# Deferred low parts in three norms, early gains, and a new order of three projections in a two-layer transformer kernel

## The chip, the cores and the metric

The kernel runs on one core of a Trainium2 chip. The metric is the device time of one execution in microseconds (us), the lower the better. The engines are named as in the profile: PE is TensorE (its weight loads are shown as PEld), DVE is VectorE, ACT is ScalarE, POOL is GpSimd, and SP is SyncE, which issues most of the DMAs. A queue name with a q at its end (SPq, POOLq) is the sequencer of that engine.

## The reference, cut to what matters

Two layers run one after the other on 512 tokens of 1024 features. The first mixes a sparse attention with a state-space scan. The second mixes a band attention with a gated delta rule and ends in a retrieval of experts (PEER). Three places matter here.

```python
def modulate(h, shift, scale):                    # and the same in layer 1
    return h * (1.0 + scale) + shift
h = modulate(rms_norm_2(x, norm1_gain), shift1, scale1)      # norm of layer 2
h2 = modulate(rms_norm_2(x, norm2_gain), shift2, scale2)     # norm before PEER
proj = h @ w_in                                   # qa, ka, va, qkv_b, z_b, ...
o_a = chunked_band_attention(qa, ka, va, ...)     # norms qa and ka per head, then attends
o_att = sparse_attention(...) * jax.nn.silu(z_att)           # layer 1, 8 heads
```

In the band attention the queries and the keys are normalized per head of 64; the values go in as they are. The gated delta rule needs, for each tile of 128 tokens, the inverse of a unit triangular matrix for each of its four heads.

## The kernel before, in words

**Products in three parts.** Every matrix product keeps float32 accuracy with three passes: a matrix is split into a high part (`hi`, `wh`) and a low part (`lo`, `wl`), and PE multiplies high by high, high by low and low by high. `wload` (L57) loads a block of weights into one of four `wr` buffers through SP, ACT copies the high part (L51), and DVE subtracts it to get the low part (L52), or POOL does if `eng` says so. There are three buffers for each part, so splits run up to three blocks ahead of their products. `gemm_t` (L76) gives a transposed result with 512 columns to each product (L72 to L74); `gemm_n` (L87) gives one row tile of 128 tokens to each of four PSUM buffers "g", of which the pool has four (L98 to L100). `gemm_n` walks over four blocks of weights with four row tiles in each, 96 products in all, and calls `mid` after every second row tile, eight times in all.

**Norms.** `norm_mod` (L210) runs three times: at the start of layer 1 (8 blocks of 128 features, fed while the modulation weights still arrive: `pre(k)` multiplies two of their blocks, L194), at the start of layer 2, and before PEER. For each block k it makes `y` (L220, DVE), the high part (L221, ACT) and the low part (L222, DVE, which needs the high part). There are three buffers for `y`. Layer 2 loads its gain at its own start (L883) and multiplies it with the modulation (L884); the norm before PEER does the same (L1273, L1274).

**Layer 1, attention.** `ssd_pre` makes eight projections with their low parts on POOL. Beside them DVE runs the top-k rounds of the indexer (L483, L484), which `pump` hands out. Then `att1_head` (L516) runs for eight heads, each beginning with a `gemm_t` of `w_za`.

**Layer 2, band projections.** `dn_pre` makes the delta rule's projections, `dn_tiles([0, 1])` inverts the matrices of the first two tiles, and `band_pre` (L1166) makes the three band projections with `gemm_n` while it hands out the rounds of `dn_tiles([2, 3])` through `mid`. One round is one step of both tiles. There are 19 with work in them: five that build the matrices, twelve that alternate between L1054 (with the transposes L1043) and L1063 for six levels, counting the first transpose, then the last results L1068 and L1074. Before: half the values (`w_va1`, 256 columns, 0.5 of a round per call), then queries and keys (512 columns each, 0.9 of a round per call). Each of the last two ends with a chain for four row tiles: copy out of PSUM (L1194, ACT), square (L1196), sum (L1198), power of -0.5 on POOL (L151), multiply (L1200), all in buffers "cv_u" and "cv_t", two each. `trans` (L1177) then transposes on PE (L1181) and copies with a scale (L1183). The queries are transposed after the keys' products; the keys' transposes are tied behind the last L1054 (`issue_after`).

**After that.** `band` (L1205) loads a bias for each head (L1215; POOL writes a corner, L1216), multiplies queries by keys (L1220) and runs a softmax on DVE and ACT (`soft`, L534), interleaved with the scan of the delta rule.

**What sets the order.** The code is a program without waits. At build time a planner fixes the order of the instructions on each engine: by its own estimate of durations it takes, at each moment, the ready instruction that stands earliest in the program. On the chip each engine runs its own list in order and waits where an input is late. The order in the program is thus a priority, not yet the order that runs.

Of the kernel before, what the change touches and what calls it, by code (L numbers as in the profile page):

```python
# [8 lines left out]
F32 = mybir.dt.float32  # L9
# [5 lines left out]
AF = mybir.ActivationFunctionType  # L15
OP = mybir.AluOpType
# [4 lines left out]
P = 128  # L21
T = 512
NT = 4
# [3 lines left out]
class Kernel:  # L27
# [181 lines left out]

    def norm_mod(self, pool, xs, hs, G, shift, ss, pre=None, mid=None):  # L210


        nc = self.nc
        r = self.rstd_bcast(pool, ss, 1.0 / 1024, "nm", pre is None, mid)
        for k in range(8):
            y = self.t(pool, [P, T], F32, "nm_y", 3)
            hi, lo = hs[k]
            if pre is not None:
                pre(k)
            nc.vector.scalar_tensor_tensor(y, xs[k], G[:, k:k + 1], r, op0=OP.mult, op1=OP.mult)  # L220
            nc.scalar.activation(hi, y, AF.Identity, bias=shift[:, k:k + 1])  # L221
            nc.vector.scalar_tensor_tensor(lo, y, shift[:, k:k + 1], hi.bitcast(F32), op0=OP.add, op1=OP.subtract)  # L222

    def run(self):
        tc, nc = self.tc, self.nc
# [133 lines left out]
    def att1_pre(self, hs):  # L359
        tc, nc, I = self.tc, self.nc, self.i  # L360
        ap, a0 = self.ap, self.ap0
        self.rope_tables(a0)
        G = nc.gpsimd

# [150 lines left out]

    def att1_head(self, h, hs):  # L516
        nc, ap = self.nc, self.ap
        z = self.gemm_t(self.i["w_za"][h], 8, hs)
        tz = self.t(ap, [P, T], F32, "tz", 1)
        nc.scalar.activation(tz, z, AF.Tanh, scale=0.5)  # L520
        zz = self.t(ap, [P, T], F32, "zz", 2)
        nc.vector.scalar_tensor_tensor(zz, tz, 1.0, z, op0=OP.add, op1=OP.mult)
        kv = h // 4
        o = self.t(self.pa, [P, T], F32, "a")
        for i in range(NT):
            N = P * (i + 1)
            s = self.t(self.pa, [P, T], F32, "a")[:, :N]
            nc.tensor.matmul(s, self.qT[h][:, i * P:i * P + P], self.kT[kv][:, :N], start=True, stop=True)
            self.soft(s, N, self.mask[i], P ** -0.5, o[:, i * P:i * P + P], lambda sb: self.v[:, sb, kv * P:kv * P + P])
        g = self.t(ap, [P, T], F32, "og", 1)  # L530
        nc.vector.scalar_tensor_tensor(g, o, 0.5, zz, op0=OP.mult, op1=OP.mult)
        nc.sync.dma_start(self.oatt_d[h], g)
# [317 lines left out]
    def mod_rest(self, pool):  # L850

        nc, cp = self.nc, self.cp
        mod2 = self.mod2 = cp.tile([P, 48], F32, tag="mod2", name="mod2")
        acc = cp.tile([P, 48], F32, tag="acc2", name="acc2")
        ab1 = self.load(pool, "ada_b", [P, 24])
        ab2 = self.load(pool, "ada_b2", [P, 48])
        cur = {}

        def blk(cname, wname, b, out, ab):
            if cname not in cur:  # L860
                c = self.t(self.wp, [P, 1024], F32, "wr", 4)
                nc.sync.dma_start(c, self.i[cname])
                s = self.t(pool, [P, 1024], F32, "sc2")
                nc.scalar.activation(s, c, AF.Tanh, scale=0.5)
                nc.vector.tensor_scalar(s, s, 0.5, 0.5, op0=OP.mult, op1=OP.add)
                nc.vector.tensor_mul(s, s, c)
                cur[cname] = s
            w = self.t(self.wp, [P, 1024], F32, "wr", 4)
            nc.sync.dma_start(w, self.i[wname][b])
            nc.vector.scalar_tensor_tensor(w, w, 1.0, cur[cname], op0=OP.mult, op1=OP.mult, accum_out=acc[:, b:b + 1])  # L870
            if b % 8 == 7:
                r = slice(b - 7, b + 1)
                nc.vector.tensor_add(out[:, r], acc[:, r], ab[:, r])

        self.bg = [lambda b=b: blk("c_b", "ada_w", b, self.mod1, ab1) for b in range(16, 24)]
        self.bg += [lambda b=b: blk("c_b2", "ada_w2", b, mod2, ab2) for b in range(48)]

    def layer2(self, st0):
        tc, nc, I = self.tc, self.nc, self.i
        cp, mod2 = self.cp, self.mod2  # L880
        with ExitStack() as st:
            lp = self.lp = st.enter_context(tc.tile_pool(name="lp", bufs=1, reuse_waits="tile"))
            G = self.load(lp, "norm1_g2", [P, 8])  # L883
            nc.vector.scalar_tensor_tensor(G, mod2[:, 8:16], 1.0, G, op0=OP.add, op1=OP.mult)  # L884
            with tc.tile_pool(name="hp2", bufs=1, side="right", reuse_waits="tile") as hp:
                hs = [(self.t(hp, [P, T], F32R, f"hh{k}"), self.t(hp, [P, T], F32R, f"hl{k}")) for k in range(8)]
                with tc.tile_pool(name="np2", bufs=1, reuse_waits="tile") as np2:
                    self.norm_mod(np2, self.x1, hs, G, mod2[:, 0:8], self.ss)
                sd = ExitStack()
                self.dk = sd.enter_context(tc.tile_pool(name="dk", bufs=1, reuse_waits="tile"))  # L890
                with tc.tile_pool(name="dp", bufs=1, reuse_waits="tile") as self.dp:
                    self.dn_pre(hs)
                    for _ in self.dn_tiles([0, 1]):
                        pass
                    tiles = self.dn_tiles([2, 3])
                    self.owed = 0.0

                    def mid(n):

                        self.owed += n  # L900
                        while self.owed >= 1.0:
                            self.owed -= 1.0
                            next(tiles, None)

                    self.band_pre(hs, mid)
                    for _ in tiles:
                        pass
                with tc.tile_pool(name="bp", bufs=1, side="right", reuse_waits="tile") as bp:
                    self.bp = self.ap = bp
                    scan, band = self.dn_scan(), self.band()  # L910
                    zb = self.zb(hs)
                    for _ in scan:
                        next(band)
                        next(band)
                    for _ in band:
                        pass
                    next(zb)
                    parts = [self.pair(bp, x, "pr", "pts", 4) for x in self.oa]
                    out = self.dn_out()
                    for _ in zb:  # L920
                        next(out)
                    for _ in out:
                        pass
                    sd.close()
                    self.out2(parts)
# [240 lines left out]
    def band_pre(self, hs, mid):  # L1166
        nc, I, lp, dp = self.nc, self.i, self.lp, self.dp
        G = nc.gpsimd
        ps = self.gemm_n(I["w_va1"], 256, hs, mid=lambda: mid(0.5))
        for t in range(NT):  # L1170
            nc.scalar.activation(self.va[:, t, 256:], ps[t], AF.Copy)
        gq = self.load(dp, "attn_qk_g", [P, 2])
        nc.vector.tensor_scalar(gq[:, 0:1], gq[:, 0:1], 0.125, None, op0=OP.mult)
        sh = [P, 8, 64]
# [10 lines left out]

        xs = None
        for j, w in enumerate(("w_qa", "w_ka")):
            ps = self.gemm_n(I[w], 512, hs, mid=lambda: mid(0.9))
            if j:
                trans(0, xs)  # L1190
            xs = []
            for t in range(NT):
                x = self.t(dp, sh, F32, "cv_u" if t % 2 else "cv_t", 2)
                nc.scalar.activation(x, ps[t].rearrange("p (h d) -> p h d", h=8), AF.Copy)  # L1194
                sq = self.t(dp, sh, F32, "qn_d", 1)
                nc.vector.tensor_mul(sq, x, x)  # L1196
                s = self.t(dp, [P, 8], F32, "bn_s", 2)
                nc.vector.tensor_reduce(s, sq, axis=AX.X, op=OP.add)  # L1198
                r = self.rstd_small(dp, s, 1.0 / 64, "bn")
                nc.vector.tensor_mul(x, x, r.unsqueeze(2).to_broadcast(sh))  # L1200
                xs.append(x)
        with self.tc.issue_after(self.mm.ins):
            trans(1, xs)

# [51 lines left out]
    def peer(self, st):  # L1256
        tc, nc, I = self.tc, self.nc, self.i
        cp = self.cp
# [11 lines left out]
        x2n_d = self.dr.tile([NT, P, 1024], F32, tag="x2n_d", name="x2n_d")  # L1270
        g2r = self.g2r = self.t(pp, [P, 1024], F32, "g2r")
        with tc.tile_pool(name="np3", bufs=1, reuse_waits="tile") as np3:
            G = self.load(np3, "norm2_g2", [P, 8])  # L1273
            nc.vector.scalar_tensor_tensor(G, mod2[:, 32:40], 1.0, G, op0=OP.add, op1=OP.mult)  # L1274
            self.x2n_d = x2n_d

            def mid():
                for t in range(2):
                    self.x2_rows(np3, t)

            self.norm_mod(np3, self.x2, hs, G, mod2[:, 24:32], self.ss, mid=mid)
            for t in range(2, NT):
                self.x2_rows(np3, t)
# [519 lines left out]
```

## Time and profile before

| what | value |
|---|---|
| three runs | 2551.0, 2552.95, 2554.04 us |
| median | 2552.95 us |
| the profiled execution's own time | 2555.68 us |
| its span, first to last instruction | 2554.0 us |
| mean granted TensorE clock | 0.976 |

The span is 1.7 us shorter than the time of the same execution, and that execution is 2.7 us above the median of the runs. Times inside the trace are counted from the start of the span. A row of the timeline gives the start, the duration and, in brackets, how long the engine sat idle before it and what ended the wait. Matmuls overlap: two that start 0.23 us apart may each last 0.39 us.

### The profile page before, as it was taken

How to read it: one execution, taken by the hardware profiler on the slowest of the kernel's cores; microseconds unless marked ns; L12 is line 12 of the kernel's file. 1: busy time of each engine (PE TensorE's matmuls, PEld its weight loads, DVE VectorE, ACT ScalarE, POOL GpSimd, SP SyncE). 2: the span in 40 equal slices, each digit the busy share in tenths (PEclk: the TensorE clock that was granted, in tenths of full speed). 3: DMA queues.
4: the chain of work that ended last, by engine and by line, in shares of the span. 5: the costliest groups of instructions: out<-in, count | busy, mean ns of one | idle time of the engine just before them, and what ended most of it. 6: DMA issues, size and time to landing. Idle time of an engine off the chain costs nothing. (4 is left out here: it accounts for less than half of the span.)

```text
span 2554.0 us, 34662 instructions
## 1 busy us (share of the span) xinstructions
PE 2431.2 (95%) x12529; PEld 2035.4 (80%) x12529; DVE 1877.0 (73%) x3627; ACT 1046.2 (41%) x1872; POOL 680.3 (27%) x517
## 2 busy tenths in 40 slices
PE   5999999999999999899998978999899999999999
PEld 4777777778788779767778878999888888888887
DVE  7895677767754784455427899998777878888887
ACT  3444466653322444344434333444333333333332
POOL 0240011120001014321104556211453434444431
PEclk8999999999999899999999999999999999999999
DMA  7222222238865211111422466799999999989995
GB/s 250 75 77 85 75 64 78 78 98 294 287 220 175 91 53 47 58 38 58 130 83 83 145 190 198 273 340 325 335 314 330 333 336 344 351 304 343 328 343 207
DMA packets 199597, 500.43 MB, mean 196 GB/s; under 512 B 20097, under 2 KB 85889, under 8 KB 196353
## 3 DMA queue, kind: packets, MB, share of 16 engines
q1 hardware_dynamic: 159104, 338.81, 40.0%
q0 software_dynamic: 36864, 134.23, 14.8%
q10 hardware_dynamic: 3456, 25.17, 2.4%
q8 instruction: 98, 1.61, 0.3%
q14 instruction: 75, 0.61, 0.1%
HBM read 448.01 MB, written 50.14 MB: 195 GB/s over the span
## 5 line engine op out<-in xcount | busy, mean ns | idle before, releaser
L51 ACT ACTIVATE wh<-wr 128x1024 fp32r<-128x1024 f32 (+2 forms) x424 | 442.5, 1046 | 613.4 <-PE g L73 317.3
L72 PE MATMUL g<-hh,wh 128*128 128x384 f32 (+1 forms) x1792 | 665.2, 371 | 19.4 <-ACT act L1643 13.9
L74 PE MATMUL g<-hh,wl 128*128 128x384 f32 (+1 forms) x1792 | 661.4, 369 | 22.3 <-POOL wl L52 18.9
L73 PE MATMUL g<-hl,wh 128*128 128x384 f32 (+1 forms) x1792 | 660.8, 369 | 0.0
L52 DVE TENSOR_TENSOR wl<-wr,wh 128x1024 fp32r<-128x1024 f32 (+2 forms) x360 | 439.9, 1223 | 167.5 <-ACT wh L51 165.2
L74 PEld LDWEIGHTS g<-hh,wl 128*128 128x128 f32 x1792 | 342.9, 191 | 60.7 <-POOL wl L52 21.7
L72 PEld LDWEIGHTS g<-hh,wh 128*128 128x128 f32 x1792 | 343.2, 192 | 56.0 <-ACT act L1643 14.4
L73 PEld LDWEIGHTS g<-hl,wh 128*128 128x128 f32 x1792 | 342.9, 191 | 39.6 <-issue 9.3
L73 PE MATMUL acc<-wl,gh 128*128 128x512 f32 x768 | 304.2, 396 | 0.0
L74 PE MATMUL acc<-wh,gl 128*128 128x512 f32 x768 | 304.1, 396 | 0.0
L72 PE MATMUL acc<-wh,gh 128*128 128x512 f32 x768 | 304.1, 396 | 0.0
L1680 POOL DMA_INDIRECT row<-in_rows_dn,idx x128 | 168.1, 1313 | 358.9 <-DVE row L1686 307.4
L1680 POOL DMA_INDIRECT row<-in_rows_up,idx x128 | 175.6, 1372 | 268.4 <-DVE gacc L1699 242.6
L52 POOL TENSOR_TENSOR wl<-wr,wh 128x1024 fp32r<-128x1024 f32 x64 | 157.2, 2464 | 239.7 <-ACT wh L51 230.8
L51 ACT ACTIVATE gh<-ga 128x384 fp32r<-128x384 f32 x128 | 67.3, 525 | 331.6 <-issue 196.4
L1686 DVE SCALAR_TENSOR_TENSOR row<-row,h2n 128x1024 f32<-128x1024 f32 x128 | 165.9, 1306 | 24.0 <-DMA row<-in_rows_dn,idx 23.7
L1699 DVE SCALAR_TENSOR_TENSOR gacc<-row,gw,gacc 128x1024 f32<-128x1024 f32 x127 | 162.7, 1281 | 13.3 <-DMA row<-in_rows_up,idx 12.4
L74 PEld LDWEIGHTS acc<-wh,gl 128*128 128x128 f32 x768 | 144.8, 189 | 34.4
L73 PEld LDWEIGHTS acc<-wl,gh 128*128 128x128 f32 x768 | 144.8, 189 | 34.0
L72 PEld LDWEIGHTS acc<-wh,gh 128*128 128x128 f32 x768 | 144.8, 188 | 34.0
L52 DVE TENSOR_TENSOR gl<-ga,gh 128x384 fp32r<-128x384 f32 x128 | 73.3, 573 | 53.7 <-ACT gh L51 53.7
L98 PE MATMUL g<-wh,hh 128*128 128x512 f32 (+3 forms) x256 | 97.0, 380 | 16.5 <-ACT hh L221 16.3
(550 smaller groups left out, 3808.1 us busy)
## 6 DMA issues: line engine op xcount, KB each, us to landing
wr<-in_w_dn SPq DMA_DIRECT2D x128, 512.0 KB, 5.0
wr<-in_w_up SPq DMA_DIRECT2D x128, 512.0 KB, 7.1
wr<-in_ada_w SPq DMA_DIRECT2D x56, 512.0 KB, 4.5
g_d<-stage ACTq DMA_DIRECT2D x24, 1024.0 KB, 8.4
gr<-g_d SPq DMA_DIRECT2D x32, 768.0 KB, 10.8
wr<-in_w_x SPq DMA_DIRECT2D x24, 512.0 KB, 3.6
act_d<-act SPq DMA_DIRECT2D x63, 192.0 KB, 4.9
ar<-act_d SPq DMA_DIRECT2D x63, 192.0 KB, 6.5
```

Source lines behind the costliest of these rows:

```text
L51: nc.scalar.activation(hi, src, AF.Copy)
L52: eng.tensor_sub(lo, src, hi.bitcast(F32))
L72: mm(ps, ah, bh, start=first, stop=False)
L73: mm(ps, ah, bl, start=False, stop=False)
L74: self.mm = mm(ps, al, bh, start=False, stop=last)
L98: mm(pss[t], hh[:, tt], wh[:, k], start=f, stop=False)
L1680: nc.gpsimd.indirect_dma_start(r, None, src, bass.IndirectOffsetOnAxis(ap=self.idx[:, s:s + 1], axis=0))
L1686: nc.vector.scalar_tensor_tensor(r, r, 1.0, self.h2n, op0=OP.mult, op1=OP.mult, accum_out=act[:, s:s + 1])
L1699: nc.vector.scalar_tensor_tensor(acc, r, w[:, s:s + 1], acc, op0=OP.mult, op1=OP.add)
```

## The change

In `norm_mod` the low part of block k is issued behind `y` and the high part of block k + 1, the last one at the end. The first head's `w_za` is split on POOL and not on DVE. The gains of the two later norms are loaded in `mod_rest`, whose other small loads are issued by 566.7 us, some 270 us ahead of the norm of layer 2, into the pool that lives as long as the kernel. In `band_pre` the half of the values moves from the first place to the last, behind the keys' chain and ahead of the keys' transposes. The rounds per call change from 0.5, 0.9, 0.9 (values, queries, keys) to 0.8, 0.8, 0.65 (queries, keys, values).

```diff
@@ norm_mod
+        last = None
+        def low(k, y):
+            nc.vector.scalar_tensor_tensor(hs[k][1], y, shift[:, k:k + 1], hs[k][0].bitcast(F32), op0=OP.add,
+                                           op1=OP.subtract)
         for k in range(8):
             y = self.t(pool, [P, T], F32, "nm_y", 3)
-            hi, lo = hs[k]
             if pre is not None:
                 pre(k)
             nc.vector.scalar_tensor_tensor(y, xs[k], G[:, k:k + 1], r, op0=OP.mult, op1=OP.mult)
-            nc.scalar.activation(hi, y, AF.Identity, bias=shift[:, k:k + 1])
-            nc.vector.scalar_tensor_tensor(lo, y, shift[:, k:k + 1], hi.bitcast(F32), op0=OP.add, op1=OP.subtract)
+            nc.scalar.activation(hs[k][0], y, AF.Identity, bias=shift[:, k:k + 1])
+            if last is not None:
+                low(k - 1, last)
+            last = y
+        low(7, last)
@@ att1_head
-        z = self.gemm_t(self.i["w_za"][h], 8, hs)
+        z = self.gemm_t(self.i["w_za"][h], 8, hs, eng=None if h else nc.gpsimd)
@@ mod_rest
+        self.gains = [self.load(cp, f"norm{j}_g2", [P, 8]) for j in (1, 2)]
@@ layer2
-            G = self.load(lp, "norm1_g2", [P, 8])
+            G = self.gains[0]
@@ band_pre
-        ps = self.gemm_n(I["w_va1"], 256, hs, mid=lambda: mid(0.5))
-        for t in range(NT):
-            nc.scalar.activation(self.va[:, t, 256:], ps[t], AF.Copy)
 ...
-            ps = self.gemm_n(I[w], 512, hs, mid=lambda: mid(0.9))
+            ps = self.gemm_n(I[w], 512, hs, mid=lambda: mid(0.8))
 ...
+        ps = self.gemm_n(I["w_va1"], 256, hs, mid=lambda: mid(0.65))
+        for t in range(NT):
+            nc.scalar.activation(self.va[:, t, 256:], ps[t], AF.Copy)
         with self.tc.issue_after(self.mm.ins):
             trans(1, xs)
@@ peer
-            G = self.load(np3, "norm2_g2", [P, 8])
+            G = self.gains[1]
```

## Rows read from the trace of the kernel before

**Rows 1.** The page: busy us, share of the span and instructions of each engine.

```profile
PE 2431.2 (95%) x12529; PEld 2035.4 (80%) x12529; DVE 1877.0 (73%) x3627; ACT 1046.2 (41%) x1872; POOL 680.3 (27%) x517
```

**Rows 2.** PE's waits, whole span: waiting line, releaser, us in total, times, longest.

```profile
PE g L74 <- POOL wl L52: 18.9, 9, 9.1
PE g L98 <- ACT hh L221: 16.3, 6, 5.8
...
PE a L1181 <- DVE cv_t L1200: 8.5, 2, 6.0
...
PE a L138 <- DVE c_norm_g L884: 2.2, 1, 2.2
```

**Rows 3.** Windows of the band projections: stretch, length, busy by engine, granted clock, DMA.

```profile
935.00:957.00 22.00, 20.88 (x151) 19.14 (x150) 19.41 (x28) 12.27 (x29) 2.78 (x2) 1.00 0.16 50
...
952.00:954.40 2.40, 2.40 (x22) 2.24 (x20) 2.40 (x4) 1.62 (x2) 1.17 (x1) 1.00 0.00 0
...
987.00:1067.50 80.50, 80.00 (x501) 70.45 (x500) 38.63 (x47) 30.58 (x54) 30.52 (x20) 1.00 0.19 60
...
1071.10:1077.30 6.20, 0.18 (x2) 0.00 (x0) 2.88 (x6) 3.15 (x7) 2.01 (x1) 0.91 0.52 170
1077.30:1094.70 17.40, 13.20 (x55) 10.23 (x55) 6.89 (x13) 3.35 (x5) 5.69 (x5) 0.54 0.01 1
```

**Rows 4.** Timeline of PE behind the keys' products, which end at 1067.46.

```profile
1067.46 1.95 PE L1063 MATMUL a<-Y,Z 128*128 128x128 f32 x16
1069.24 0.60 PE L1181 MATMUL a<-ident,cv_t 128*128 128x128 f32 x4
...
1077.31 1.12 PE L1181 MATMUL a<-ident,cv_t 128*128 128x128 f32 x4 [6.02 <-DVE cv_t L1200]
```

**Rows 5.** Timeline of the keys' chain and the bias loads; last, the loads' landing.

```profile
1070.85 0.90 SPq L1215 DMA_DIRECT2D bias<-in_rel_bias  x2
...
1072.18 0.61 ACT L1194 ACTIVATE cv_t<-g 128x512 f32<-128x512 f32 x1
...
1074.52 2.01 POOL L151 TENSOR_TENSOR bn_r<-bn_v,mhalf 128x8 f32<-128x8 f32 x1 [18.85 <-DVE bn_v L147]
...
1076.56 0.69 DVE L1200 TENSOR_TENSOR cv_t<-cv_t,bn_r 128x512 f32<-128x512 f32 x1 [1.53 <-POOL bn_r L151]
...
1087.09 0.69 DVE L1200 TENSOR_TENSOR cv_u<-cv_u,bn_r 128x512 f32<-128x512 f32 x1 [1.81 <-POOL bn_r L151]
...
bias<-in_rel_bias SPq DMA_DIRECT2D x4, 256.0 KB, 3.2
```

**Rows 6.** Timeline of DVE: the queries' chain, beside the keys' products.

```profile
1030.59 1.65 DVE L1200 TENSOR_TENSOR cv_u<-cv_u,bn_r 128x512 f32<-128x512 f32 x1 [1.53 <-POOL bn_r L151]
```

**Rows 7.** Timeline by engine, and one window, around the first head's `w_za` products.

```profile
178.28 2.51 POOL L52 TENSOR_TENSOR wl<-wr,wh 128x1024 fp32r<-128x1024 f32 x1 [8.44 <-ACT wh L51]
...
183.63 1.99 ACT L51 ACTIVATE wh<-wr 128x1024 fp32r<-128x1024 f32 x2
...
188.73 1.21 DVE L52 TENSOR_TENSOR wl<-wr,wh 128x1024 fp32r<-128x1024 f32 x1
...
189.99 0.79 PE L74 MATMUL g<-hh,wl 128*128 128x512 f32 x1 [3.25 <-DVE wl L52]
...
194.67 1.22 DVE L52 TENSOR_TENSOR wl<-wr,wh 128x1024 fp32r<-128x1024 f32 x1
...
190.00:195.30 5.30, 5.30 (x13) 4.13 (x14) 5.30 (x10) 1.77 (x3) 0.00 (x0) 0.50 0.31 99
```

**Rows 8.** Timeline of the norms of layer 1 (first row) and layer 2.

```profile
48.24 1.23 DVE L194 SCALAR_TENSOR_TENSOR adw<-adw,sc 128x1024 f32<-128x1024 f32 x1 [2.43 <-DMA adw<-in_ada_w]
...
837.98 0.16 DVE L884 SCALAR_TENSOR_TENSOR c_norm_g<-mod,c_norm_g 128x8 f32<-128x8 f32 x1
...
840.29 2.07 DVE L220 SCALAR_TENSOR_TENSOR nm_y<-e,c_norm_g,a 128x512 f32<-128x512 f32 x3 [2.15 <-PE a L138]
...
841.85 0.59 PE L98 MATMUL g<-wh,hh 128*128 128x264 f32 x1 [1.60 <-ACT hh L221]
```

## The prediction

> **What bounds the kernel now.** I read the page first: PE is busy for 2431.2 of 2554.0 us [rows 1], so all work that moves inside a busy stretch of PE is worth nothing, and a gain can only come from the 123 us in which PE waits or from stretches at the low clock. Then PE's waits by line [rows 2]: the reader sees 16.3 us for high parts of a norm (L98 behind L221), 8.5 us for the keys' multiply (L1181 behind L1200), 2.2 us put down to a gain (L884). Then windows and timelines at the changed places.
>
> The band projections [rows 3]: from 987.0 to 1067.5, with products and rounds together, PE idles 0.5 us in 80.5. Behind it comes a hole: from 1071.1 to 1077.3 PE works 0.18 us, and until 1094.7 it is busy 13.20 of 17.40 us at a mean granted clock of 0.54 of full, between its levels of 1.2 and 2.4 GHz, after an idle stretch of 6 us. The timeline names the cause [rows 4, 5]: the keys' transposes wait for a chain of four row tiles, serial because the square has one buffer, from 1072.18 to 1087.78, which is 15.6 us. Nothing else is left for PE except one round and the first scores.
>
> At the first head of layer 1, PE stops 3.25 us for a low part that DVE begins only at 188.73, though its high part was done by 185.62 at the latest [rows 7]; the 13 products behind it run at clock 0.50 (1.2 GHz) until 195.3.
>
> **The change, part by part.**
>
> *Values last.* The values' 96 products and the six last rounds of tiles 2 and 3 now lie between the keys' copies and their transposes. The count of rounds stays: 0.5, 0.9, 0.9 times eight calls gives 18.4, now 0.8, 0.8, 0.65 gives 18.0; 12 of them are out when the keys' products end. Cover for the chain: 22 products of 256 columns took 2.40 us [rows 3], so 96 take 10.5. A round takes at least the 1.78 us of its 16 L1063 products, 1067.46 to 1069.24 [rows 4]; six are 10.7. Together 21 us against 15.6, or 19.4 if all four multiplies take 1.65 us as the one beside POOL's work did, and not 0.69 [rows 5, 6]. So the chain ends under PE's work, by a margin of 2 to 6 us. What leaves the path: 6.20 - 0.18 = 6.0 us, and 17.40 - 13.20 x 0.54 = 10.3 us in the second window, where I take the work at full clock since nothing idles before it. Together **-16.3**.
>
> What is late next. (a) The values' products need PSUM that the keys' copies free, and these need "cv_t" and "cv_u", which the queries' transposes free. The copies began 2.9 us after the first transpose (1072.18 against 1069.24), behind four scaled copies on ACT, the same queue; PE's transposes cover 1.8 of that, and the copy itself takes 0.6, so PE lacks 1.7 us unless the planner puts the 13th round there, which is ready. 0 to 1.7. (b) DVE waits 1.53 us for POOL's power in each row tile, in its own order [rows 5]; a tile round's L1064 behind it waits too, and PE for that: 0 to 4 x 1.53 = 6.1. The queries' chain ran in the same company and all of PE's idle time there was 0.5 [rows 3, 6]. (c) The first bias is issued 3.4 us after the last product (1070.85) and lands 3.2 us later [rows 5], 20 us ahead of its use. Now PE's rest (two sets of transposes or level products of 1.8 us and two of L1068 and L1074 of the same counts, 7 us) is all that covers those 6.6: 0 to 2. Nearest row is the queries' 0.5 for (b), and some of (a) and (c): I take **+3**, ends 0 and 9.8. (d) On SP the values' four loads, 256 KB each, pass behind eight of 512 KB and ahead of the later weights; the DMA share in the stretch is 0.19 [rows 3], so they are free. (e) DVE is busy 19.41 of 22.0 us in 935 to 957 and PE idles 1.1 there; the queries' blocks are twice as long to split, but their products fill PE: -1.1 to +1.1, taken as 0.
>
> *First split on POOL.* POOL's split takes 2.51, DVE's 1.21 [rows 7]. POOL has nothing after 180.8, so it may start when ACT has the high part: with the first of its two splits, at 184.7, and end at 187.2. PE wants it at 186.7: a wait of 0.5 instead of 3.25. The low clock, behind the long wait, costs its 13 products 5.30 x 0.50 = 2.65; behind the short one I take full clock. Gross 5.4. But the second head's low part stays on DVE (194.67 to 195.8); DVE saves 1.2, so it is there at 194.6, while PE, 24 products on, would like it at some 193. PE waits there again. Ends: -1.2 (only DVE's queue counts) and -5.4; I take **-3**.
>
> The Trainium skill (GPSIMD Engine Reference, Performance versus the Vector engine) says that VectorE does two-input elementwise work about twice as fast and should keep it; the rows agree on the ratio (2.51 against 1.21). The rule speaks against this edit: by it the sum would be that of R4 below, where DVE's late start counts for nothing.
>
> *Low parts deferred.* In layer 2 the planner already runs three `y` before the first low part [rows 8], since that low part is not ready earlier; and from the first product at 841.85 PE waits for nothing until the norm is over, so a block's high part coming earlier has no taker. Bounds: a low part of one block is 0.7 us of DVE, so -0.7 to +0.7 in layer 1, where 16.3 us of waits stand [rows 2]. These are paced by the modulation weights: DVE itself waits 2.43 us for one [rows 8]. The low part now sits behind that wait, and PE's products of it may meet the next high part. In the third norm I see no more than that either. Taken as 0; the loss and the gain have the same ends.
>
> *Gains early.* L884 takes 0.16 us and stands behind the matrix that PE really needs, so of the 2.2 us in rows 2 at most 0.16 can go. 0. The two SP issues move into a stretch where nothing waits for them.
>
> Sum: -16.3 + 3 - 3 = -16.3 against the profiled execution's own 2555.68 gives 2539.4. That execution is 2.7 above the median; against 2552.95 it is 2536.7. Behind these places PE is bound by its work, so the rest only moves forward.
>
> **The rivals.**
>
> *R1, the chain is not covered.* The cover's margin is 2 to 6 us, and the planner fixes PE's place for the transposes by its own estimate. If the chain stretches and PE waits some 6 us again, half the clock gain goes too (5): -16.3 + 6 + 5 - 3 = -8, 2545. For it: the contended 1.65 [rows 6]. Against: 0.5 us in 80.5 [rows 3]. The Trainium skill (SBUF, Who interferes with whom) makes the pair of ports that DVE and POOL share an exclusive lock for two-input DVE work; eight of the chain's instructions would each be open to it, as the one long multiply shows.
>
> *R2, the planner wins already.* The order in the program is only a priority. If it places the products as before, only the split is left: 2550. Against: PSUM has four "g" buffers and each product takes all, so the three projections must run in program order.
>
> *R3, slower.* One mechanism: POOL's in-order queue. Each power (2.0 us) now stands between the rounds' own POOL work, and DVE's wait behind it holds the round's subtraction. If all four serialize, 4 x (2.0 + 1.53 + 0.96 of stretch) = 18 us, and at half clock over the stretch of 21 us of work as much as 21 more: -16.3 + 18 + 21 - 3 = +20, 2573. It decides once these waits pass 19 us in total; the queries' chain cost 0.5 in the same company.
>
> *R4, the split is the loss.* If POOL begins no earlier than DVE did (its queue holds something that the trace doesn't show, or the weights land late), the part ends 2.51 - 1.21 = 1.3 us later than before: 2552.95 - 16.3 + 3 + 1.3 = 2541. Against: POOL stands idle after 180.8. It is the case that the Trainium skill's rule above describes.
>
> **How the numbers follow.** About 0.2% (5.1 us) is what a measurement of this kernel can tell from no change. Forecast 0.73; R1 0.11; R2 0.05; R3 0.06; R4 0.05. The forecast's own range: best -16.3 - 5.4 - 1.1 - 0.7 - 0.4 = -24, 2529; worst -16.3 + 9.8 - 1.2 + 1.1 + 0.7 = -6, 2547. R1 and R4 lie inside or near it; with 2 us for R1's upper half the range is 2529 to 2549. Faster by over 0.2% (below 2547.8): 0.72 of the forecast's 0.73, 0.07 of R1 and R4's 0.05, together 0.84. Within: 0.01 of the forecast, 0.04 of R1 and R2's 0.05, 0.10. Slower: R3, 0.06.
>
> **What would show it.** In the new trace: no idle stretch of PE over 2 us between the keys' products and the first scores, and clock 1.00 there; L1181's wait for L1200 gone from PE's waits; the keys' chain beside products of 256 columns; the first L74 of `w_za` behind POOL with under 1 us of wait, and a new wait of 1 to 2 us one head later; norms as long as before. I am wrong if PE idles at the start of the values or ahead of the keys' transposes, if the hole only moves to the first softmax, or if a later stretch gets longer.

## The result, and the profile after

The changed kernel takes 2521.4 us (2519.0 to 2522.4) against 2552.9 for the kernel before on the same chip: a ratio of 0.9876, with a 95% interval from 0.9859 to 0.9893. That is 31.4 us, about twice the 16.3 that were forecast, and below the stated range.

First the page of the changed kernel, its busy times and clock; they answer to [rows 1].

```profile
span 2520.7 us, 34660 instructions
PE 2409.1 (96%) x12529; PEld 2031.1 (81%) x12529; DVE 1870.2 (74%) x3626; ACT 1045.7 (41%) x1872; POOL 685.2 (27%) x518
```

The reader is to see that PE does the same 12,529 matmuls in 22 us less busy time. A change that only removed waits would leave the busy time where it was, but for the stretches at half clock. By the mean granted clocks of the two executions (0.976 of 2554.0 us, 0.979 of 2520.7) these account for at most 61 - 53 = 8 us, 6 of them in the band's hole (13.20 x 0.46, [rows 3]). So something made the products themselves shorter, and no step of the prediction had that.

The waits of PE in the changed kernel (waiting line, releaser, us in total, times, longest); they answer to [rows 2].

```profile
PE g L74 <- POOL wl L52: 18.7, 10, 8.9
PE g L98 <- ACT hh L227: 11.4, 5, 3.2
...
PE a L559 <- DVE pr L555: 8.6, 5, 5.9
...
PE a L1064 <- DVE bn_v L147: 4.2, 2, 2.5
```

The keys' multiply is gone from the list. New are 5.9 us of one softmax (L559 behind L555) and 4.2 us in two pieces of a tile round (L1064).

The band, which answers to [rows 3, 4]: windows of the changed kernel, then PE's timeline there.

```profile
987.00:1040.00 53.00, 52.17 (x314) 45.52 (x313) 30.09 (x39) 18.45 (x34) 24.03 (x16) 1.00 0.13 41
1040.00:1066.00 26.00, 21.55 (x165) 20.73 (x164) 15.72 (x23) 10.92 (x19) 12.81 (x8) 0.93 0.13 41
1066.00:1080.00 14.00, 14.00 (x123) 13.72 (x121) 5.58 (x7) 8.62 (x15) 0.00 (x0) 1.00 0.46 148
1080.00:1096.00 16.00, 15.43 (x93) 10.69 (x92) 10.72 (x52) 9.30 (x29) 3.72 (x7) 1.00 0.13 35
```

```profile
1074.42 0.60 PE L1188 MATMUL a<-ident,cv_t 128*128 128x128 f32 x4
...
1080.04 4.34 PE L1230 MATMUL g<-e,e 64*128 64x128 f32 x16
...
1085.13 0.48 PE L1230 MATMUL g<-e,e 64*128 64x128 f32 x2 [0.49 <-DVE mx L548]
```

The hole is closed: from 1066 to 1080 PE works all 14.00 us at full clock, and the keys' transposes (L1188) wait for nothing. The price stands earlier, between 1040 and 1066, where PE idles 26.00 - 21.55 = 4.45 us, 2.5 of them in one wait, and the mean clock is 0.93.

Last the accumulating products of the final stage (L72 to L74 into `acc`), which no part of the change touches: groups by line and shape from 1900 to 2500 us, with count, busy us and mean ns, first of the kernel before and then of the changed one.

```profile
L72 PE MATMUL acc<-wh,gh 128*128 128x512 f32 x668 | 264.5, 396 | 0.0
L73 PE MATMUL acc<-wl,gh 128*128 128x512 f32 x667 | 264.2, 396 | 0.0
L74 PE MATMUL acc<-wh,gl 128*128 128x512 f32 x667 | 264.1, 396 | 0.0
```

```profile
L72 PE MATMUL acc<-wh,gh 128*128 128x512 f32 x686 | 266.9, 389 | 0.0
L73 PE MATMUL acc<-wl,gh 128*128 128x512 f32 x685 | 266.7, 389 | 0.0
L74 PE MATMUL acc<-wh,gl 128*128 128x512 f32 x685 | 266.6, 389 | 0.0
```

In both kernels PE is busy there for all but 0.3 us of the 600, at full clock, yet one product takes 396 ns before and 389 after. The 2304 of them in the kernel (768 on each line) make 2304 x 0.007 = 16 us, the size of what was missing. The timelines say the same from start to start: 2199.72, 2199.95, 2200.18, 2200.41, 2200.65 before, some 233 ns apart, and 2170.19, 2170.41, 2170.64, 2170.87, 2171.09 after, some 226. (The Trainium skill, TensorE: Matmul & The Clock Gate, Back-to-back issue gap, has two figures for 512 columns: some 216 ns as the gap of a product by itself, and some 131 ns for a sustained stream with a weight load for each. Neither kernel reaches either.)

### The profile page after: what moved, and what is told of

It reads as the page before. It is cut to its first block, busy times and chain, and to the rows that moved or that the text cites. A ratio compares the mean times of both kernels' runs of the same rounds, so it can differ in the third digit from the quotient of the medians.

```text
span 2520.7 us, 34660 instructions
## 1 busy us (share of the span) xinstructions
PE 2409.1 (96%) x12529; PEld 2031.1 (81%) x12529; DVE 1870.2 (74%) x3626; ACT 1045.7 (41%) x1872; POOL 685.2 (27%) x518
## 5 line engine op out<-in xcount | busy, mean ns | idle before, releaser
L72 PE MATMUL g<-hh,wh 128*128 128x384 f32 (+1 forms) x1792 | 662.4, 370 | 15.7 <-ACT act L1653 10.2
L74 PE MATMUL g<-hh,wl 128*128 128x384 f32 (+1 forms) x1792 | 656.7, 366 | 18.7 <-POOL wl L52 18.7
L52 DVE TENSOR_TENSOR wl<-wr,wh 128x1024 fp32r<-128x1024 f32 (+3 forms) x359 | 438.1, 1222 | 162.0 <-ACT wh L51 161.1
L74 PEld LDWEIGHTS g<-hh,wl 128*128 128x128 f32 x1792 | 341.5, 191 | 56.8 <-POOL wl L52 22.4
L72 PEld LDWEIGHTS g<-hh,wh 128*128 128x128 f32 x1792 | 341.4, 191 | 51.9 <-ACT act L1653 11.0
L73 PE MATMUL acc<-wl,gh 128*128 128x512 f32 x768 | 299.0, 389 | 0.0
L74 PE MATMUL acc<-wh,gl 128*128 128x512 f32 x768 | 298.9, 389 | 0.0
L72 PE MATMUL acc<-wh,gh 128*128 128x512 f32 x768 | 298.8, 389 | 0.0
L72 PEld LDWEIGHTS acc<-wh,gh 128*128 128x128 f32 x768 | 144.2, 188 | 29.9
L74 PEld LDWEIGHTS acc<-wh,gl 128*128 128x128 f32 x768 | 144.2, 188 | 29.8
L98 PE MATMUL g<-wh,hh 128*128 128x512 f32 (+3 forms) x256 | 97.1, 382 | 11.9 <-ACT hh L227 11.4
```

The lines of the kernel that those rows point to most:

```text
L52: eng.tensor_sub(lo, src, hi.bitcast(F32))
L72: mm(ps, ah, bh, start=first, stop=False)
L73: mm(ps, ah, bl, start=False, stop=False)
L74: self.mm = mm(ps, al, bh, start=False, stop=last)
L98: mm(pss[t], hh[:, tt], wh[:, k], start=f, stop=False)
```

## The experiments

No line of the last stage was changed, but the place of its tiles in SBUF was. The change loads the two gains, 32 bytes each per partition, into pool `cp`, which is allocated from the low end and lives throughout. Everything allocated behind them moves up by 64 bytes, the weights `wh` and `wl` among them; `hh`, `hl`, `gh` and `gl` lie in pools at the high end and stay. The addresses that the two programs assign (bytes in a partition), and their rest modulo 256:

```
            before           changed kernel
wh          36256  (160)     36320  (224)
hh         196576  (224)    196576  (224)
gh         136160  (224)    136160  (224)
ysh        120256  (192)    120320  (  0)
ph          87488  (192)     87552  (  0)
```

So theory A: the place of the weights against the other operand sets the time of a product. Theory B: the shorter products come from the new order of the work.

**The shift alone.**

```diff
+        self.pad = cp.tile([P, 16], F32, tag="pad", name="pad")
```

> The kernel before with one unused tile of 64 bytes per partition, taken where the change takes its two gains (which are 32 bytes each). Nothing else differs: every tile that the program allocates from the low end after it, the weight buffers wh and wl among them, lies 64 bytes higher; hh, hl, gh and gl, allocated from the high end, stay. Theory A (the place of the weights in SBUF, against that of the other operand, sets the time of a product of 512 columns): the 2304 accumulating products of the last stage start 227 ns apart instead of 233, which is 14 us, and the 2300 of 512 columns with hh and the 480 of the normed rows give up to 8 more; 2531 to 2539 us. Theory B (the shorter products come from the new order of the work, not from the place): the products keep their 231 and 236 ns, and the time stays within 0.2% of 2552.9.

It took 2531.6 us, ratio 0.9919 (0.9906 to 0.9932): 21.4 us from a tile that nothing reads or writes. Its group of L72 from 1900 to 2500 us:

```profile
L72 PE MATMUL acc<-wh,gh 128*128 128x512 f32 x686 | 266.9, 389 | 0.0
```

Every engine runs the same instructions in the same order as in the kernel before, so theory B is out.

**The gains as before, all else changed.** The weights fall back to 36256.

```diff
-        self.gains = [self.load(cp, f"norm{j}_g2", [P, 8]) for j in (1, 2)]
...
-            G = self.gains[0]
+            G = self.load(lp, "norm1_g2", [P, 8])
...
-            G = self.gains[1]
+            G = self.load(np3, "norm2_g2", [P, 8])
```

> The changed kernel with the gains of the two norms loaded where the kernel before loads them: the one part that also undoes the shift of 64 bytes. Theory A: the products of the last stage fall back to 231 and 236 ns, and 14 to 22 us of the 31.4 are lost; 2535 to 2543 us. Theory B: only the early load is lost, 0.16 us for the one instruction of DVE that stands behind it; 2521.5 within 0.2%.

2539.3 us, ratio 0.9945 (0.9931 to 0.9958): 17.8 us lost against 2521.4 (ratio 0.9876). The `acc` products are back at 395 to 396 ns. What the other three parts give together is 2553.0 - 2539.3 = 13.7 us.

**The band order alone.** Beside these lines the three of the values' projection move behind the loop, as in the change.

```diff
-        ps = self.gemm_n(I["w_va1"], 256, hs, mid=lambda: mid(0.5))
...
-            ps = self.gemm_n(I[w], 512, hs, mid=lambda: mid(0.9))
+            ps = self.gemm_n(I[w], 512, hs, mid=lambda: mid(0.8))
...
+        ps = self.gemm_n(I["w_va1"], 256, hs, mid=lambda: mid(0.65))
```

> The kernel before with the band projections in the order queries, keys, values and the changed rates of rounds, nothing else; the weights stay where they were. If the values cover the keys' chain as in the changed kernel, PE gains 12 to 16 us between the last product of the keys and the first scores, and nothing elsewhere: 2537 to 2541 us. If the gain there belonged to the shift or to another part: 2548 or more. The products of the last stage stay at 231 and 236 ns.

2540.7 us, ratio 0.9948 (0.9935 to 0.9962), 12.3 us less. The traces put it a little lower: from the start of PE's 4000th matmul to that of its 5600th, which takes in the whole stretch, the seven kernels with the old order take 280.9 to 282.3 us and this one 271.2. From 1066 to 1080 PE is busy all 14.00 us, at a clock of 0.89, and the waits between 930 and 1110 are those of the changed kernel:

```profile
PE a L1054 <- DVE bn_v L147: 4.4, 2, 2.5
PE a L1054 <- DVE X L1064: 0.5, 1, 0.5
PE g L1220 <- DVE mx L539: 0.5, 1, 0.5
```

**The split back on DVE.**

```diff
-        z = self.gemm_t(self.i["w_za"][h], 8, hs, eng=None if h else nc.gpsimd)
+        z = self.gemm_t(self.i["w_za"][h], 8, hs)
```

> The changed kernel with the first head's split back on DVE. In the changed kernel PE wins 5 us at the products of w_za and then stands 5.88 us at the first transposes of the softmax, where DVE comes late; from 158 to 325 us of the span it loses 1.7 us against the kernel before. If the split on POOL only moves the wait: the same time within 0.1%, or up to 2 us faster. If it is a gain of 3 us as forecast: 2524.5 us. The first w_za low part is then waited for by some 3 us, and the softmax transposes by under 1.

2519.6 us (2517.0 to 2532.2) against 2521.4 with the split on POOL; the ratios to the kernel before are 0.9877 (0.9858 to 0.9897) and 0.9876. Times with intervals of 4 to 5 us to either side can't tell 0 from the 3 us of the forecast, but the traces can. From the start of PE's 500th matmul to that of its 1600th, which takes in this place, eight of the eleven kernels with the split on DVE take 228.9 or 229.0 us and the other three up to 231.7; the two with the split on POOL take 230.6 (the changed kernel) and 230.2 (the one with the gains as before). POOL gains nothing. PE's waits from 180 to 206 us, with the split on POOL (the changed kernel) and then on DVE:

```profile
PE a L559 <- DVE pr L555: 5.9, 1, 5.9
PE g L74 <- POOL wl L52: 0.6, 1, 0.6
```

```profile
PE g L74 <- DVE wl L52: 3.4, 1, 3.4
PE a L559 <- DVE pr L555: 1.9, 1, 1.9
```

6.5 us of waits in the one, 5.3 in the other. PE is through the products of `w_za` sooner and then stands at the first head's transposes, since DVE comes no sooner: the windows of the changed kernel there (busy of PE, PEld, DVE, ACT, POOL; clock) show DVE full, and the half clock behind the wait.

```profile
188.00:198.00 10.00, 4.13 (x20) 3.10 (x19) 9.69 (x18) 5.95 (x15) 0.00 (x0) 0.92 0.36 113
196.00:204.00 8.00, 5.99 (x18) 4.83 (x19) 3.08 (x11) 2.43 (x7) 0.00 (x0) 0.57 0.22 68
```

**The deferral alone.** The kernel before with the new loop of the norms.

```diff
...
+            if last is not None:
+                low(k - 1, last)
+            last = y
+        low(7, last)
```

> The kernel before with the low parts of the norms deferred, nothing else; the weights stay where they were. As forecast (0 with ends of 0.7 us to either side): 2552.9 within 0.7 us. If the first norm gains by it what the changed kernel shows there (the longest wait of PE for a high part 3.2 us instead of 5.8, the norm ends 3.1 us earlier, of which the shift alone gave 1.8 by the same place): 1.3 to 3 us less, 2550 to 2551.6.

2551.0 against 2552.0 us, ratio 0.9994 (0.9979 to 1.0009): not to be told from nothing. In the first norm (18 to 60 us) PE's wait for high parts differs: before, with the deferral alone, and in the kernel with a tile of 32 bytes (below), whose norms have the old loop:

```profile
PE g L98 <- ACT hh L221: 14.7, 5, 5.8
```

```profile
PE g L98 <- ACT hh L227: 11.1, 4, 4.1
```

```profile
PE g L98 <- ACT hh L221: 9.1, 4, 3.0
```

So the fall from 14.7 to 11.1 can't be put down to the deferral. In the seven traces with the old loop this wait is 9.1 to 15.0 us, in the six with the new one 9.8 to 11.1.

**The other operand moved instead.** An unused tile of 64 bytes at the high end; the weights stay, `hh`, `hl`, `gh` and `gl` go down to 160 modulo 256, where the weights are.

```diff
+            hz = st.enter_context(tc.tile_pool(name="hz", bufs=1, side="right"))
+            self.hz = hz.tile([P, 16], F32, tag="hz", name="hz")
```

> The kernel before with an unused tile of 64 bytes per partition at the other end of SBUF, so that hh, hl, gh and gl lie 64 bytes lower and the weights stay. Theory A1 (the place of the two operands against each other counts): both lie at 416 modulo 512, the products with hh and the accumulating ones take 227 ns, and the time is that of the run with the low tile, 2529 to 2534 us. Theory A2 (each operand's own place counts, 480 modulo 512 or some divisor is good): the products stay at 231 to 236 ns, 2553 within 0.3%. The products with ysh and ph stay slow by both.

2528.9 us, ratio 0.9908 (0.9887 to 0.9928), `acc` products at 389 ns. Those with `ph` and `ysh`, whose distance from the weights is as before, keep their 233 ns from start to start. No address is good in itself; the place of the operands against each other counts.

**24 offsets.** Unused tiles of 32 bytes between the pairs of `ph` and `ysh` in the kernel before; the pairs get letters in place of numbers.

```diff
...
+                self.t(op, [P, 8], F32, f"q{tag}{c}")
                 hi = self.t(op, [P, T], F32R, f"{tag}h{c}")
```

> The kernel before with unused tiles of 32 bytes between the pairs ph, pl and ysh, ysl of layer 1's last products, so that the 24 pairs stand at 24 offsets against the weights, from 64 to 800 bytes in steps of 32 (pha at 64, phg at 256, ysha at 320, yshg at 512, ysho at 768). In the kernel before all of them stand at 32 modulo 512 and take 233 to 234 ns. Theory A1 with a period of 256: phg, yshg and ysho take 227 ns, all others more. With a period of 128: also phc, yshc and yshk. With a period of 512: yshg alone. The time is that of before, within 3 us. Theory A2 or B: no such order.

A miss: none of the places that theory A1 names is fast. The groups of L72 from 680 to 830 us, at 64, 192, 256, 512 (`yshg`) and 320 (`ysha`); the same line takes 395 to 396 ns there in the kernel before:

```profile
L72 PE MATMUL g<-pha,wh 128*128 128x512 f32 x8 | 3.2, 399 | 0.0
...
L72 PE MATMUL g<-phg,wh 128*128 128x512 f32 x8 | 3.2, 397 | 0.0
...
L72 PE MATMUL g<-phe,wh 128*128 128x512 f32 x8 | 3.1, 391 | 0.0
...
L72 PE MATMUL g<-yshg,wh 128*128 128x512 f32 x6 | 2.4, 397 | 0.0
...
L72 PE MATMUL g<-ysha,wh 128*128 128x512 f32 x6 | 2.3, 388 | 0.0
```

Offsets that differ by 256 repeat each other (391 at 192, 448 and 704; 394 at 128, 384 and 640), but 0 is not fast where the neighbours on both sides stand 32 bytes off. The exception is `ysha` at 320, with 388 the fastest, where `pha` and `yshi` at 64 take 399: seven of the eight `ysha` products of L72 follow a product with `hh`, which stands at 64 too. So the product just before may count as well. The one run took 2548.0 us.

**Six groups of four pairs with one offset each.**

```diff
+                gap = {"pa": 24, "pe": 32, "ysa": 64, "yse": 16, "ysi": 8, "ysm": 24}.get(tag + c)
+                if gap:
+                    self.t(op, [P, gap], F32, f"q{tag}{c}")
...
```

> The 24 offsets gave no pair its 227 ns, not even those at 256, 512 and 768; only stages whose operands all stand at one place modulo 512 are fast so far. So here neighbours share an offset: the pairs of layer 1's last products in six groups of four (twelve products in a row), at 128 (pha), 256 (phb), 0 modulo 512 (ysha), 64 (yshb), 96 (yshc) and 192 (yshd) against the weights. Theory A1a (the offset counts modulo 256, and the product before must share it): phb and ysha take 227 ns but for the products at a group's edge, the other groups 230 to 236. Modulo 512: ysha alone. Modulo 128: pha too. Theory A1b (the whole stage, also what is further away, must share one place): no group is fast. The time: that of before less 0.8 us (128 products of 6.5 ns) for each group that is fast.

Groups from 680 to 830 us, at 128, 256, 192, 96, 64 and 0:

```profile
L72 PE MATMUL g<-pha,wh 128*128 128x512 f32 x32 | 12.6, 394 | 0.0
...
L72 PE MATMUL g<-phb,wh 128*128 128x512 f32 x32 | 12.5, 390 | 0.0
...
L72 PE MATMUL g<-yshd,wh 128*128 128x512 f32 x28 | 11.0, 394 | 0.0
...
L72 PE MATMUL g<-yshc,wh 128*128 128x512 f32 x27 | 10.7, 395 | 0.0
L72 PE MATMUL g<-yshb,wh 128*128 128x512 f32 x24 | 9.5, 395 | 0.0
...
L72 PE MATMUL g<-ysha,wh 128*128 128x512 f32 x24 | 9.3, 390 | 0.0
```

As theory A1a has it: 256 and 0 are fast, 64, 96, 128 and 192 are not, and a pair needs neighbours of its own offset. From start to start, over whole groups and worked out as in the next experiment, the products are 228.4 ns apart at 0 and at 256, 230.5 at 64, 232.8 at 128 and 192, and 234.1 at 96. The one run took 2550.6 us; a gain of 1.6 us is below what one run can show.

**32 bytes in place of 64.**

```diff
+        self.pad = cp.tile([P, 8], F32, tag="pad", name="pad")
```

> The kernel before with an unused tile of 32 bytes in place of the 64: the weights stand 32 bytes below hh and gh modulo 512, which is half of their distance in the kernel before. If only the same place is fast, the accumulating products take 231 to 236 ns as before, 2553 within 0.3%; if the loss grows with the distance, some 230 ns and half the gain of 21 us, 2540 to 2545.

A miss to the slow side: 2564.1 us, ratio 1.0035 (1.0019 to 1.0051). The `acc` products stay at 395 ns, and those with `hh`, which had been partly fast at an offset of 64, lose the rest. Groups of L74 from 250 to 540 us, in the kernel before and in this one:

```profile
L74 PE MATMUL g<-hh,wl 128*128 128x512 f32 x256 | 103.5, 404 | 0.0
```

```profile
L74 PE MATMUL g<-hh,wl 128*128 128x512 f32 x256 | 103.8, 405 | 0.0
```

These means hold stretches at half clock, so they understate it; at full clock the starts of the products with `hh` are 229.7 ns apart on the mean in the kernel before, 233.2 here and 228.4 in the changed kernel, worked out from all gaps of 150 to 300 ns between starts of the three traces that lie outside the half clock. Over 2304 products the 3.5 ns are 8 us. Half the distance is no half way.

**All operands in one place.** The changed kernel with the split on DVE and 224 bytes ahead of the tiles of pool `op`, which brings `ph` and `ysh` to the weights' 224 modulo 256.

```diff
+        self.op_pad = op.tile([P, 56], F32, tag="op_pad", name="op_pad")
         self.mod_rest(op)
```

> The changed kernel with the first head's split on DVE (which was worth nothing) and ph and ysh moved by 224 bytes, so that they stand at 480 modulo 512 like the weights. Theory A1: 768 products fall from 233.5 to 227 ns, 5 us; 2514 to 2517 us against 2519.6 for the same kernel without the move and 2521.4 for the changed one. Theory A2 or B: 2519.6 within 0.1%.

2515.6 us, ratio 0.9858 (0.9836 to 0.9879), the lowest median of all. The 4 us against 2519.6 lie inside the intervals of the two; the products show the gain more clearly, 233 ns from start to start in the changed kernel and 226.5 to 227.1 here. Groups from 680 to 830 us in the changed kernel and in this one:

```profile
L72 PE MATMUL g<-ysh,wh 128*128 128x512 f32 x103 | 40.7, 395 | 0.0
L72 PE MATMUL g<-ph,wh 128*128 128x512 f32 x64 | 25.3, 395 | 0.0
```

```profile
L72 PE MATMUL g<-ysh,wh 128*128 128x512 f32 x98 | 38.1, 389 | 0.0
L72 PE MATMUL g<-ph,wh 128*128 128x512 f32 x64 | 24.9, 389 | 0.0
```

**Fewer rounds beside the queries' chain.** The same kernel with other rates.

```diff
-            ps = self.gemm_n(I[w], 512, hs, mid=lambda: mid(0.8))
+            ps = self.gemm_n(I[w], 512, hs, mid=lambda: mid(0.55 if j else 0.8))
...
-        ps = self.gemm_n(I["w_va1"], 256, hs, mid=lambda: mid(0.65))
+        ps = self.gemm_n(I["w_va1"], 256, hs, mid=lambda: mid(0.9))
```

> The last kernel (2515.6 us: the changed one with the split on DVE and ph, ysh at the weights' place) with the rates of rounds 0.8, 0.55 and 0.9 in place of 0.8, 0.8 and 0.65: two of the rounds that ran beside the queries' chain now run beside the values. In the changed kernel PE waits 4.2 us in two pieces for a round's product, whose operand DVE delivers behind the chain's waits for POOL. If those waits come from the rounds' place beside the chain, they go and the end of the keys' chain keeps its cover: 2 to 4.5 us less between 930 and 1110 us of the span, some 2512 us. If the chain waits for POOL beside any round: no change there, 2515.6 within 0.1%, with the waits beside the values or the keys' chain.

A miss: 2521.5 us, ratio 0.9879 (0.9862 to 0.9895). PE's waits between 920 and 1110 us, with the old rates and the new:

```profile
PE a L1065 <- DVE bn_v L147: 4.2, 2, 2.5
```

```profile
PE a L1065 <- DVE bn_v L147: 5.5, 2, 3.2
```

From PE's 4000th matmul to its 5600th this kernel takes 274.0 us against 270.2 with the old rates. In both, the two waits stand behind the queries' transposes, among the values' products and so beside the keys' chain, which is where the new rates put two more rounds. This way of spreading the rounds is worse; the other way, fewer rounds beside the values, wasn't tried.

## Why the prediction was wrong, step by step

**Gains early: the step that failed.** It read: at most 0.16 can go, 0, and the two issues move into a stretch where nothing waits. It priced the instructions of the edit and not its tiles. The gains came into a pool that lies ahead of every other at the low end, and that moved the weights by 64 bytes against `hh` and `gh`. By the run with the empty tile this is worth 21.4 us, by the run that undoes it 17.8. The gaps from start to start, worked out as above, give its size: 15 us from the 2304 `acc` products (233.3 to 226.8 ns), 3 from the 2304 of 512 columns with `hh` (229.7 to 228.4), and 2.7 from the 480 that stream `wh` in the norms and projections (L98 to L100; 233.3 to 227.7): 21.

**Values last: right, and nearly in size.** -16.3 + 3 = -13.3 was forecast, 12.3 measured by the times (9.7 to 16.6) and 10 to 11 by the traces. The hole is gone as described. The three waits, for which I took 3 with ends 0 and 9.8: (a) shows as 0.2 us (L98 behind the keys' copy), (c) as 0.5 at most, at the second head's scores, and (b), a round's product behind DVE's waits for POOL, is 4.2 of its bound of 6.1. The sum had no term for the clock behind (b): 0.93 over 26 us is another 26 x 0.07 = 1.8 us. So the signs "no idle stretch of PE over 2 us" and "clock 1.00" did not come true, and the queries' 0.5 was a poor guide for (b). (That there PE has 12 products of 512 columns, 2.8 us, to each call of `mid`, and beside the keys' chain 12 of 256, 1.4 us, may be why; no run shows it.) That (b) hangs on the chain's waits for the power, 1.53 us each [rows 5], is read from DVE's order and wasn't taken away by a run; with two more rounds there (rates 0.55 and 0.9) the waits grew from 4.2 to 5.5.

**First split on POOL: 3 us forecast, 0 measured.** The near end was right: a wait of 0.64 where 0.5 stood, and no half clock behind it. What came next was sized wrongly. I looked for the next wait at the second head's products, with 1 to 2 us; it came at the first head's own softmax with 5.88, behind a DVE that is busy 9.69 of 10.00 us, and the half clock came with it (0.57). So the split is worth nothing, though not by R4's way: POOL did begin early, at 180.50 us and nearly 5 us ahead of DVE's own next split, and DVE's queue decided. The Trainium skill's rule (GPSIMD Engine Reference, Performance versus the Vector engine) that such work belongs on VectorE is borne out as to the result, not as to its reason.

**Low parts deferred: 0 forecast, 1.1 measured with an interval across zero.** The interval goes from 5.4 us less to 2.3 more and holds the forecast with its 0.7 to either side. In the changed kernel PE waits less for high parts in the first norm (9.8 us against 14.7), against the sign "norms as long as before"; but kernels with the old loop show waits as short, so no run tells what the deferral does there.

**The sum.** Band 12.3, shift 17.8 to 21.4, deferral about 1, split 0: 31 to 35 us against 31.4. Without the shift the forecast of 2537 stands against 2539.3. Those 2 to 3 us too few are the split's 3 and the band's 1 to 3, less what the deferral may have given. In the range's best end, 0.4 us has no row behind it.

**The rivals.** R1, R2, R3 and R4 did not come: the chain is covered, the values' products run behind the keys' on PE, the serializing cost 4.2 us where R3 needed 19, and POOL began early.

## What to carry to other kernels

When an edit allocates, look at what it moves: compare the addresses of the operands of the costliest products before and after, since a tile that nothing reads made 2304 products 6.5 ns shorter each. Where products of 512 columns in fp32r fill PE, try the stationary and the moving operand at the same place modulo 256 bytes, in the whole stage; here 224 empty bytes brought 768 more products from 233 to 227 ns. And when a wait is removed from a chain, look for the next one in the same chain first: the engine that was late is late still.

## What the runs showed of the hardware

A product of 128x512 in this kernel is followed by the next after 227 to 228 ns on the mean when all operands of the stage share one place modulo 256 bytes, and after 230 to 234 when they don't. An offset of 32 cost as much as any (233 ns with `hh`); one of 64 cost less there (229.7), but with `gh`, where `wh` is the operand that streams, as much as 32 did (396 and 395 ns for one product). Products of 384 columns gain nothing: at full clock they start 173.4 ns apart in the kernel before, where `hh` stands at 64, and 173.7 in the changed one. (That their means on L72 fall from 347 to 345 ns is no gain either: these means hold stretches at half clock.) Pairs at the right place between neighbours 32 bytes off were not fast. What in the memory does this stays open: no run here looked inside, and why 64 bytes cost `acc` more than `hh` wasn't tried; the two differ in which operand streams, and with it in the sign of the offset.
